# Weights split in 512-column halves, a split-ahead of three products, and a staged, earlier preparation of the token-side sums in a seven-product gate stage

## The chip, the cores and the metric

The kernel runs on one NeuronCore of a Trainium2 chip (eight cores, two dies). The metric is the device time of one execution in microseconds (us). The core's engines run side by side and meet through semaphores: PE (TensorE: matmul, with its weight loads listed apart as PEld), DVE (VectorE), ACT (ScalarE), POOL (GpSimd) and SP (SyncE), which here issues every DMA. Each engine takes its own instructions in the order in which the program issues them.

## The reference

Two layers (DEPTH 2) work on x of 1024 tokens by 1024 channels. Five branches read the same normalised input h; each gives a 1024 x 256 result `yb`; then they are merged:

```python
merged = None
for n, yb in enumerate((y_hg, y_cf, y_sc, y_at, y_mem)):
    term = jax.nn.sigmoid(h @ w_gate[l, n]) * (yb @ w_branch[l, n])
    merged = term if merged is None else merged + term
x = x + rmsnorm(merged @ w_out[l], norm_post[l])
```

`h @ w_gate[l, n]` is a 1024 x 1024 by 1024 x 1024 product for each of five branches and two layers; `h @ w_in[l]` is 1024 x 4352, `yb @ w_branch` 256 x 1024 for each branch. The rest of a layer is a bidirectional linear recurrence (branch 0), a 31-tap depthwise convolution with a layer norm (1), a 3-tap one (2), windowed attention (3) and attention into 256 memory tokens (4). All arrays are float32.

## The kernel before

**Precision.** A float32 product is made of three matmuls in the float32r form. Each operand is split into `hi` (a rounding copy, by ACT) and `lo = x - hi` (a subtraction, by DVE) in `split` (L336); `mm3` adds hi.hi, lo.hi and hi.lo in one PSUM bank. So every weight tile costs one ACT copy and one DVE subtraction before PE can use it, and every 128 x 128 x 512 block of the product costs three matmuls.

**Weights.** `split_w` (L351) makes a `raw` tile (one of four) and issues its load at once; its inner `done` later makes a `hi` and a `lo` tile of 1024 columns (two buffers each) and issues the split. Called with `own`, it takes two long-lived `slot` tiles in their place.

**Items and look-ahead.** `program` (L1459) yields Items, each with a `prep` (issue the loads) and a `body` (issue the matmuls and what reads their result). `drive` (L452) works one item at a time: before an item's body it calls `done` of the next item (the split), then `prep` of the one after that. `plan.wait(need)` holds an item back until a named flag is up.

**The planner.** All five engines are under a manual schedule: the order in which Python issues instructions is the order in which each engine runs them. `Planner` (L117) keeps one clock per engine from rough costs (`Meter`). Work beside the items is a generator handed to `plan.side`: it issues one stage, then yields. After every three matmuls `poll` (L181) issues the next stage of each side whose last stage is finished, by the planner's clocks, at the planner's present PE time. `wait` and `idle` move the planner's PE time on to the next due side; real PE doesn't wait there, only the order of issue is set.

**Buffers.** Long-lived tiles come from 38 `slot`s of 128 x 1024. Short-lived ones of 128 x 512 come from eight `h2` buffers: the terms of the token-side sums, the output copies `pb_out`, the thresholds `th`, and `g_s1`, `g_e`, `g_u` of the gates. A buffer is taken over when every reader of the tile before is done, a DMA included. PSUM has four banks (`mm`) for the items.

**The end of a layer.** After the five branches' own work come, in this order: five pairs of `branch_items` (L1084: 96 matmuls a branch; each 128 x 512 block is copied by ACT to `pb_out` and stored to DRAM as `pb`), mixed with plain gate items (branch 2, and two of branch 0). The last pieces are `cz` (two items of the convolution branch, which need flag `cf`, raised when the convolution's side `conv`, L610, has been issued to its end), one plain gate item `hg_g[1]` (flag `plain`), and the two items of branch 1 (flag `pbs` at their end). Then `strassen_items` (L1209) compute the other 15 gate blocks of 256 columns ("groups"), each as a 2 x 2 block product with seven products in place of eight, in the order P1, P6, P5, P2, P7, P3, P4, each 12 matmuls. The output items (`out_items`, L1371) follow.

**The seven products.** The weight of a group has four blocks a11, a12, a21, a22 in two raw tiles. P1 takes a11, P2 a12, P4 a22; the others take sums: s1 = a21 + a22 for P5, a11' = s1 - a11 for P6, a21' = a11 - a21 for P7, a12' = a12 - a11' for P3. `split_product` (L1227) forms these on DVE in place, when the product is split; products are split into the halves of a shared 1024-column tile pair. On the token side P1, P2 and P3 take blocks of h as they are; P5, P6, P7 and P4 take T1 to T4, sums of blocks of h, made once a layer by the side `gate_forms` (L1162): for i in 0, 1 and k in 0, 1 it rebuilds four blocks (hi + lo), forms four differences and splits them (`put`). The i = 1 half waits for `plain` (slots), its T3 and T4 for `pbs`. P6 of the first group needs flag `forms`, P7 `all_forms`. `after` (L1278) reads each product's bank, applies the gate (tanh) and adds to `mg`; in the last group `halve` (L1267) also makes the split operands of the output product.

Of the kernel before, what the change touches and what calls it, by code (L numbers as in the profile page):

```python
# [12 lines left out]
F32R = mybir.dt.float32r  # L13
# [193 lines left out]
def encoder(ctx: ExitStack, tc: tile.TileContext, a: dict, out: bass.AP):  # L207
# [142 lines left out]

    def split_w(parts, shape, name, own=False):  # L351

        raw = wp.tile(shape, F32, tag="raw", bufs=4, name=f"raw_{name}")
        for dst, src in parts(raw):
            load(out=dst, in_=src)

        def done():
            if own:
                hi, lo = (slot(f"w{v}", F32R).rearrange("p (k c) -> p k c", k=KC) for v in "hl")
            else:  # L360
                hi = wp.tile(shape, F32R, tag="hi", name=f"hi_{name}")
                lo = wp.tile(shape, F32R, tag="lo", name=f"lo_{name}")
            split(hi, lo, raw)
            return hi, lo

        return done

    def cols(l, *starts, own=False):

# [21 lines left out]
    def half_proj(hT, w, s, name):  # L391

        ps = mmt(f"ps_{name}")
        hi, lo = w
        yield from mm3(ps, [(hi[:, k, :], lo[:, k, :], hT[s][0][k // 2][:, k % 2, :], hT[s][1][k // 2][:, k % 2, :])
                            for k in range(KC)])
        return ps

# [132 lines left out]
    def memory_items(l, kv):  # L531

        mT = [None, None]
        plan.side(memory_norm(l, mT))
        src = a["w_mem_kv"][l].rearrange("(k p) c -> p k c", p=P)
        items = []
        for j in range(4):
            def parts(raw, j=j):
                return [(raw, src[:, :, j * P:(j + 1) * P])]

            def prep(j=j, parts=parts):
                return split_w(parts, [P, KC, P], f"mkv{l}{j}")

            def body(w, j=j):
                if j == 0:
                    kv["k"] = slot(f"mK{l}", F32R).rearrange("p (v j m) -> p v j m", v=2, j=2)
                    kv["v"] = small.tile([P, 2, W], F32, tag="mV", bufs=1, name=f"mV{l}")
                ps = mmt(f"ps_mkv{j}")
                yield from mm3(ps[:, :M], [(w[0][:, k, :], w[1][:, k, :], mT[0][k // 4][:, k % 4, :],
                                            mT[1][k // 4][:, k % 4, :]) for k in range(KC)])  # L550
                if j < 2:
                    split(kv["k"][:, 0, j, :], kv["k"][:, 1, j, :], ps[:, :M])
                else:
                    to_tokens(ps[:, :M], kv["v"][:, :, (j - 2) * P:(j - 1) * P])
                yield

            items.append(Item(prep, body, f"mT{l}" if j == 0 else None, f"mkv{l}" if j == 3 else None))
        return items
# [525 lines left out]
    def branch_items(l, n, ys, pbd, need=None, flag=None):  # L1084

        wb = a["w_branch"][l, n].rearrange("(j p) c -> p j c", p=P)
        yT = []
        items = []
        for q in range(2):
            def prep(q=q):  # L1090
                done = split_w(lambda raw: [(raw, wb[:, :, hs(q)])], [P, 2, HALF], f"b{n}{q}")

                def put():
                    if q == 0:
                        plan.wait(need)
                        for j, y in enumerate(ys):
                            yT.append((slot(f"yh{n}{j}", F32R), slot(f"yl{n}{j}", F32R)))
                            split(*yT[j], y)
                    return done()

                return put

            def body(w, q=q):
                for i in range(4):
                    c = slice(i * P, (i + 1) * P)
                    for s in range(2):
                        ps = mmt(f"ps_b{n}")
                        yield from mm3(ps, [(w[0][:, j, c], w[1][:, j, c], yT[j][0][:, hs(s)], yT[j][1][:, hs(s)])
                                            for j in range(2)])
                        pb = h2("pb_out")  # L1110
                        act.copy(out=pb, in_=ps)
                        load(out=pbd[4 * q + i][:, hs(s)], in_=pb)
                        yield

            items.append(Item(prep, body, flag=flag if q else None))
        return items
# [45 lines left out]
    def gate_forms(l, hT, forms):  # L1162
# [17 lines left out]
        for i in range(2):  # L1180
# [2 lines left out]
            dst, late = {}, []  # L1183
            for k in range(2):
                b11, b12, b22, b21 = (h2(f"b{x}") for x in range(4))
                for b, K, s in ((b11, 0, 0), (b12, 0, 1), (b22, 1, 1), (b21, 1, 0)):
                    hi, lo = (hT[s][v][2 * K + i][:, k, :].bitcast(F32) for v in range(2))
                    dve.tensor_tensor(out=b, in0=hi, in1=lo, op=ALU.add)
                dve.tensor_tensor(out=b11, in0=b12, in1=b11, op=ALU.subtract)
                put(dst, 1, k, b11)  # L1190
                dve.tensor_tensor(out=b12, in0=b22, in1=b12, op=ALU.subtract)
                dve.tensor_tensor(out=b22, in0=b22, in1=b11, op=ALU.subtract)
                dve.tensor_tensor(out=b21, in0=b21, in1=b22, op=ALU.subtract)
                put(dst, 2, k, b22)
                yield
                late.append((k, b12, b21))
                if i == 0 or k:
# [3 lines left out]
                    for x, j in ((3, 1), (4, 2)):  # L1201
                        for b in late:
                            put(dst, x, b[0], b[j])
                    late = []
                    yield
        plan.flags.add(f"all_forms{l}")
        yield

    def strassen_items(l, groups, forms, pbd, mg, mgd, mT):  # L1209
# [17 lines left out]
        def split_product(k):  # L1227
            gi, name = k // N, order[k % N]
            r = raws[gi]
            a11, a12, a21, a22 = r[0][:, :4], r[0][:, 4:], r[1][:, :4], r[1][:, 4:]  # L1230
            if name == "P1":
                src = a11
            elif name == "P6":
                s1 = sums[gi] = h2("g_s1").rearrange("p (k c) -> p k c", k=4)
                dve.tensor_tensor(out=s1, in0=a21, in1=a22, op=ALU.add)
                dve.tensor_tensor(out=a21, in0=a11, in1=a21, op=ALU.subtract)
                dve.tensor_tensor(out=a11, in0=s1, in1=a11, op=ALU.subtract)
                src = a11
            elif name == "P5":
                src = sums.pop(gi)  # L1240
            elif name == "P2":
                src = a12
            elif name == "P7":
                src = a21
            elif name == "P3":
                dve.tensor_tensor(out=a12, in0=a12, in1=a11, op=ALU.subtract)
                src = a12
            else:
                src = a22
                raws.pop(gi)  # L1250
            if k % 2 == 0:
                ws["tiles"] = [wp.tile([P, KC, P], F32R, tag=v, name=f"{v}_s{k}") for v in ("hi", "lo")]
            hi, lo = (t[:, 4 * (k % 2):4 * (k % 2) + 4, :] for t in ws["tiles"])
            split(hi, lo, src)
            ws[k] = hi, lo

        def merge(gi, dd, s, th):
            n, g = groups[gi]
# [19 lines left out]
        def after(k):  # L1278
# [40 lines left out]
                flush()  # L1319
                gate(gi, 1, 0, b["E1"])  # L1320
            if gi == len(groups) - 1:
                if name in ("P6", "P5", "P2"):
                    halve(("P6", "P5", "P2").index(name), 0)
                elif name == "P4":
                    flush()
                    halve(3, 0)
# [10 lines left out]
        items = []  # L1337
        for k in range(N * len(groups)):
            def prep(k=k):
                while state["loaded"] < len(groups) and N * state["loaded"] - 5 <= k:  # L1340
                    load_group(state["loaded"])
                    state["loaded"] += 1

                def done():
                    while state["split"] < N * len(groups) and state["split"] <= k + 1:
                        split_product(state["split"])
                        state["split"] += 1

# [22 lines left out]
    def out_items(l, mT, s, x_src, gpost, before, after):  # L1371
# [20 lines left out]
        for cb in range(2):  # L1392
            for q in range(4):
# [3 lines left out]
                def body(w, cb=cb, q=q):  # L1397
# [7 lines left out]
                    for i in range(4):  # L1405
                        if q == 0:
                            pss[i] = mmt("ps_o")
                        if os[i] is None:
# [2 lines left out]
                        ps = pss[i]  # L1411
                        tt = slice(i * P, (i + 1) * P)
                        yield from mm3(ps, [(mT[s][0][q][:, k, tt], mT[s][1][q][:, k, tt],
                                             w[0][:, k, :], w[1][:, k, :]) for k in range(2)],
                                       q == 0, q == 3)
                        if q == 3:
                            junk = h2("osq")
# [10 lines left out]
    with tc.manual_schedule(engines={mybir.EngineType.PE, mybir.EngineType.DVE, mybir.EngineType.Activation,  # L1428
# [30 lines left out]
        def program():  # L1459
# [22 lines left out]
            for l in range(NL):  # L1482
# [8 lines left out]
                else:  # L1491
# [13 lines left out]
                sc_g = [gate_item(l, 2, d, hT, pbd[2], mg[0], mgd[d // 2] if d > 1 else None, True, f"merge{l}")  # L1505
                        for d in range(KC)]
                hg_g = [gate_item(l, 0, d, hT, pbd[0], mg[0], None, False, f"plain{l}" if d else None) for d in range(2)]
                at_b = branch_items(l, 3, y_at, pbd[3], need=f"at{l}")
                mem_b = branch_items(l, 4, y_mem, pbd[4], need=f"mem{l}")
                yield from branch_items(l, 2, y_sc, pbd[2])  # L1510
                yield from sc_g[:1] + branch_items(l, 0, o_hg, pbd[0]) + sc_g[1:3] + at_b + sc_g[3:] + mem_b + hg_g[:1]
                yield from cz + hg_g[1:] + branch_items(l, 1, y_cf, pbd[1], flag=f"pbs{l}")
                groups = [(n, g) for g in range(4) for n in ((3, 4, 1) if g == 0 else (0, 3, 4, 1))]
                forms = {}
                plan.side(gate_forms(l, hT, forms))
                yield from strassen_items(l, groups, forms, pbd, mg, mgd, mT)
                gpost = cache(lambda l=l: row_bcast(a["norm_post"][l], f"gpost{l}"))
                x_src, hT = (x_mid if l else x_in), [None, None]
# [43 lines left out]
```

## Time and profile before

| | us |
|---|---|
| median of 3 runs (2364.68 to 2367.6) | 2365.22 |
| the profiled execution | 2366.64 |
| its span in the trace | 2364.9 |
| mean granted PE clock in the span | 0.989 |
| PE busy (share of the span) | 2276.3 (96%) |
| DVE busy | 1595.1 (67%) |
| ACT busy | 959.8 (41%) |

The span is the time from the first to the last instruction in the trace; 1.7 us of the execution lie outside it. "Busy" is the time in which an engine worked on an instruction; the views behind the page give, for each wait, the instruction that ended it. All kernel code is issued through one helper line (L112), so the views are read by tile name: `ps_b` is the bank of a branch item, `pb_out` its copy, `b` a block of h or a difference of blocks, `T1h`/`T1l` to `T4h`/`T4l` the split sums, `hi_s`/`lo_s` the split weights of a product, `raw_g` a gate weight, `ps_gX`, `ps_gY`, `ps_gZ` the three banks of a group (P1 and P2 in X; P6, P7 and P4 in Y; P5 and P3 in Z).

### The profile page before, as it was taken

The numbers are of one execution on the slowest core, as the hardware profiler recorded it, in microseconds if no ns is written. First come the engines' busy times: TensorE is split into PE (matmuls) and PEld (weight loads), VectorE is DVE, ScalarE is ACT, GpSimd is POOL, SyncE is SP. The second block draws the span as 40 slices with busy tenths as digits, with TensorE's granted clock in tenths as the row PEclk, the third lists the DMA queues.
The fourth block names the chain that finished last, engine by engine and source line by source line (L and its number), as shares of the span: only waits on it lengthen the run. The fifth ranks groups of instructions, "written<-read, shape, count | busy, mean of one in ns | idle before, by whom it ended". The sixth has DMA issues, their size and how long they took to land. (4 is left out here: it accounts for less than half of the span.)

```text
span 2364.9 us, 29886 instructions
## 1 busy us (share of the span) xinstructions
PE 2276.3 (96%) x11560; PEld 1844.3 (78%) x11560; DVE 1595.1 (67%) x2650; ACT 959.8 (41%) x1800; POOL 29.4 (1%) x41
## 2 busy tenths in 40 slices
PE   7999999999998899999999999999999988999998
PEld 6777788888887677777877778888888776777776
DVE  6768645356976777777667685453579667777765
ACT  5333344345344433334442424443543533333342
POOL 1000000000000000000110000000000000000000
PEclk9999999999999899999999999999999999999999
DMA  5210121115542333335430101111245513333334
GB/s 180 86 36 28 40 40 43 45 37 170 177 161 89 135 125 125 107 124 178 160 116 28 36 28 43 28 52 45 76 147 183 192 62 135 125 125 107 103 138 160
DMA packets 248014, 237.31 MB, mean 100 GB/s; under 512 B 29984, under 2 KB 191008, under 8 KB 247872
## 3 DMA queue, kind: packets, MB, share of 16 engines
q1 hardware_dynamic: 247872, 235.40, 30.7%
q8 instruction: 91, 1.49, 0.3%
q14 instruction: 51, 0.42, 0.1%
HBM read 177.69 MB, written 57.67 MB: 100 GB/s over the span
## 5 line engine op out<-in xcount | busy, mean ns | idle before, releaser
L112 DVE TENSOR_TENSOR lo_s<-raw_g,hi_s 128x512 fp32r<-128x512 f32 x180 | 123.9, 688 | 98.0 <-ACT hi_s L112 98.0
L112 DVE SCALAR_TENSOR_TENSOR cf_c<-cf_u,cfw,cf_c 128x1009 f32<-128x1009 f32 (+14 forms) x120 | 153.1, 1276 | 3.2
L112 ACT CAST hi_s<-raw_g 128x512 fp32r<-128x512 f32 x180 | 109.7, 617 | 92.4 <-DVE raw_g L112 88.7
L112 PE MATMUL ps_b<-yh,hi_b 128*128 128x512 f32 x320 | 129.9, 406 | 13.6 <-ACT pb_out L112 13.6
L112 PE MATMUL ps_b<-yh,lo_b 128*128 128x512 f32 x320 | 126.2, 394 | 0.0
L112 PE MATMUL ps_b<-yl,hi_b 128*128 128x512 f32 x320 | 126.2, 394 | 0.0
L112 ACT COPY pb_out<-ps_b 128x512 f32<-128x512 f32 x160 | 91.1, 591 | 68.0 <-PE ps_b L112 49.3
L112 DVE TENSOR_TENSOR lo_in<-raw_in,hi_in 128x1024 fp32r<-128x1024 f32 x60 | 73.3, 1222 | 59.8 <-ACT hi_in L112 54.6
L112 PE MATMUL ps_gX<-h_0h,hi_s 128*128 128x512 f32 x240 | 93.4, 389 | 0.0
L112 PE MATMUL ps_gX<-h_0h,lo_s 128*128 128x512 f32 x240 | 93.4, 389 | 0.0
L112 PE MATMUL ps_gX<-h_0l,hi_s 128*128 128x512 f32 x240 | 93.3, 389 | 0.0
L112 ACT ACTIVATE g_e<-g_e 128x512 f32<-128x512 f32 x60 | 38.0, 634 | 133.0 <-DVE g_e L112 133.0
L112 PEld LDWEIGHTS ps_b<-yh,hi_b 128*128 128x128 f32 x320 | 61.2, 191 | 29.1 <-ACT pb_out L112 15.3
L112 DVE TENSOR_TENSOR lo_wo<-raw_wo,hi_wo 128x1024 fp32r<-128x1024 f32 x32 | 39.0, 1224 | 59.5 <-ACT hi_wo L112 59.5
L112 PEld LDWEIGHTS h_s<-hQQ,hkp 64*128 64x128 f32 x896 | 58.9, 187 | 21.7 <-issue 14.7
L112 DVE COPY_PREDICATED hS<-masks,h_s 128x512 f32<-128x512 uint8 x112 | 75.2, 725 | 0.0
L112 PE MATMUL h_s<-hQQ,hkp 64*128 64x128 f32 x896 | 71.2, 294 | 3.4 <-ACT hkp L112 3.4
L112 ACT CAST hi_in<-raw_in 128x1024 fp32r<-128x1024 f32 x60 | 62.9, 1049 | 27.2 <-issue 26.6
L112 PEld LDWEIGHTS ps_b<-yl,hi_b 128*128 128x128 f32 x320 | 60.9, 190 | 13.2
L112 ACT COPY hkp<-hK 128x512 f32<-128x512 f32 x56 | 37.2, 665 | 83.4 <-DVE hK L112 83.4
L112 PEld LDWEIGHTS ps_b<-yh,lo_b 128*128 128x128 f32 x320 | 61.3, 192 | 11.2
L112 PE MATMUL ps_gY<-T2h,hi_s 128*128 128x512 f32 x120 | 50.8, 423 | 16.5 <-ACT T2h L112 16.5
(557 smaller groups left out, 6531.2 us busy)
## 6 DMA issues: line engine op xcount, KB each, us to landing
raw_g<-in_w_gate_dram SPq DMA_DIRECT2D x80, 512.0 KB, 3.6
pb<-pb_out SPq DMA_DIRECT2D x160, 256.0 KB, 2.3
pb<-pb SPq DMA_DIRECT2D x80, 512.0 KB, 5.0
raw_in<-in_w_in_dram SPq DMA_DIRECT2D x68, 512.0 KB, 3.8
raw_wo<-in_w_out_dram SPq DMA_DIRECT2D x32, 512.0 KB, 4.4
raw_b<-in_w_branch_dram SPq DMA_DIRECT2D x20, 512.0 KB, 5.4
mg<-g_th SPq DMA_DIRECT2D x24, 256.0 KB, 2.1
mg<-mg SPq DMA_DIRECT2D x12, 512.0 KB, 5.5
```

Source lines behind the costliest of these rows:

```text
L112: return f(*args, **kw)
```

## The change

Four things change. (1) `split_w` splits a weight in two halves of 512 columns, each with its own `hi` and `lo` tile (four buffers each), in place of one pass over 1024 columns; it now returns a list of views by k, so that the users index `w[0][k]`. (2) A product of the gate stage has its own pair of 512-column tiles, is split three products ahead (before: two), and a group is loaded one product earlier; the three block sums of a group are formed with P1's split (before: P6's), a12' with P2's (before: P3's). (3) `gate_forms` is handed to the planner before the branch items rather than after them, its stages are cut finer (sums; differences; T1 and T2; T3; T4), and the order of the sums is changed. (4) In the last group `halve` comes one product earlier.

```diff
 def split_w(parts, shape, name, own=False):
...
         def done():
-            if own:
-                hi, lo = (slot(f"w{v}", F32R).rearrange("p (k c) -> p k c", k=KC) for v in "hl")
-            else:
-                hi = wp.tile(shape, F32R, tag="hi", name=f"hi_{name}")
-                lo = wp.tile(shape, F32R, tag="lo", name=f"lo_{name}")
-            split(hi, lo, raw)
-            return hi, lo
+            n, w = shape[1:]
+            flat = raw.rearrange("p k c -> p (k c)")
+            views = [[], []]
+            for s in range(2):
+                if own and s == 0:
+                    halves = [[x[:, hs(s)] for s in range(2)] for x in (slot(f"w{v}", F32R) for v in "hl")]
+                parts = [halves[v][s] if own else split_tile(v) for v in range(2)]
+                split(*parts, flat[:, hs(s)])
+                for v in range(2):
+                    views[v] += [parts[v][:, k * w:(k + 1) * w] for k in range(n // 2)]
+            return views
+
+    def split_tile(v):
+        return wp.tile([P, HALF], F32R, tag=("hi", "lo")[v], bufs=4, name=("hi", "lo")[v])
...
 def gate_forms(l, hT, forms):
...
                 b11, b12, b22, b21 = (h2(f"b{x}") for x in range(4))
-                for b, K, s in ((b11, 0, 0), (b12, 0, 1), (b22, 1, 1), (b21, 1, 0)):
+                for b, K, s in ((b12, 0, 1), (b11, 0, 0), (b22, 1, 1), (b21, 1, 0)):
                     hi, lo = (hT[s][v][2 * K + i][:, k, :].bitcast(F32) for v in range(2))
                     dve.tensor_tensor(out=b, in0=hi, in1=lo, op=ALU.add)
+                yield
                 dve.tensor_tensor(out=b11, in0=b12, in1=b11, op=ALU.subtract)
-                put(dst, 1, k, b11)
                 dve.tensor_tensor(out=b12, in0=b22, in1=b12, op=ALU.subtract)
                 dve.tensor_tensor(out=b22, in0=b22, in1=b11, op=ALU.subtract)
                 dve.tensor_tensor(out=b21, in0=b21, in1=b22, op=ALU.subtract)
+                yield
+                put(dst, 1, k, b11)
                 put(dst, 2, k, b22)
                 yield
                 late.append((k, b12, b21))
...
                     for x, j in ((3, 1), (4, 2)):
                         for b in late:
                             put(dst, x, b[0], b[j])
+                        yield
                     late = []
-                    yield
...
 def split_product(k):
...
+            hi, lo = (split_tile(v).rearrange("p (k c) -> p k c", k=4) for v in range(2))
+            ws[k] = hi, lo
             if name == "P1":
-                src = a11
-            elif name == "P6":
                 s1 = sums[gi] = h2("g_s1").rearrange("p (k c) -> p k c", k=4)
                 dve.tensor_tensor(out=s1, in0=a21, in1=a22, op=ALU.add)
                 dve.tensor_tensor(out=a21, in0=a11, in1=a21, op=ALU.subtract)
+                split(hi, lo, a11)
                 dve.tensor_tensor(out=a11, in0=s1, in1=a11, op=ALU.subtract)
-                src = a11
+            elif name == "P6":
+                split(hi, lo, a11)
...
             elif name == "P2":
-                src = a12
+                split(hi, lo, a12)
+                dve.tensor_tensor(out=a12, in0=a12, in1=a11, op=ALU.subtract)
...
 def after(k):
...
-                if name in ("P6", "P5", "P2"):
-                    halve(("P6", "P5", "P2").index(name), 0)
+                if name in ("P1", "P6", "P5"):
+                    halve(("P1", "P6", "P5").index(name), 0)
...
             def prep(k=k):
-                while state["loaded"] < len(groups) and N * state["loaded"] - 5 <= k:
+                while state["loaded"] < len(groups) and N * state["loaded"] - 6 <= k:
...
-                    while state["split"] < N * len(groups) and state["split"] <= k + 1:
+                    while state["split"] < N * len(groups) and state["split"] <= (k + 2 if k else 1):
...
 def program():
...
+                forms = {}
+                plan.side(gate_forms(l, hT, forms))
                 at_b = branch_items(l, 3, y_at, pbd[3], need=f"at{l}")
...
                 yield from cz + hg_g[1:] + branch_items(l, 1, y_cf, pbd[1], flag=f"pbs{l}")
                 groups = [(n, g) for g in range(4) for n in ((3, 4, 1) if g == 0 else (0, 3, 4, 1))]
-                forms = {}
-                plan.side(gate_forms(l, hT, forms))
```

More of the change, by code (lines that the diff above doesn't have):

```diff
@@ L394, in half_proj @@
         hi, lo = w
-        yield from mm3(ps, [(hi[:, k, :], lo[:, k, :], hT[s][0][k // 2][:, k % 2, :], hT[s][1][k // 2][:, k % 2, :])
+        yield from mm3(ps, [(hi[k], lo[k], hT[s][0][k // 2][:, k % 2, :], hT[s][1][k // 2][:, k % 2, :])
                             for k in range(KC)])
@@ L548, in body @@
                 ps = mmt(f"ps_mkv{j}")
-                yield from mm3(ps[:, :M], [(w[0][:, k, :], w[1][:, k, :], mT[0][k // 4][:, k % 4, :],
+                yield from mm3(ps[:, :M], [(w[0][k], w[1][k], mT[0][k // 4][:, k % 4, :],
                                             mT[1][k // 4][:, k % 4, :]) for k in range(KC)])
@@ L1107, in body @@
                         ps = mmt(f"ps_b{n}")
-                        yield from mm3(ps, [(w[0][:, j, c], w[1][:, j, c], yT[j][0][:, hs(s)], yT[j][1][:, hs(s)])
+                        yield from mm3(ps, [(w[0][j][:, c], w[1][j][:, c], yT[j][0][:, hs(s)], yT[j][1][:, hs(s)])
                                             for j in range(2)])
@@ L1236, in split_product @@
                 dve.tensor_tensor(out=a21, in0=a11, in1=a21, op=ALU.subtract)
+                split(hi, lo, a11)
                 dve.tensor_tensor(out=a11, in0=s1, in1=a11, op=ALU.subtract)
-                src = a11
+            elif name == "P6":
+                split(hi, lo, a11)
             elif name == "P5":
-                src = sums.pop(gi)
+                split(hi, lo, sums.pop(gi))
             elif name == "P2":
-                src = a12
+                split(hi, lo, a12)
+                dve.tensor_tensor(out=a12, in0=a12, in1=a11, op=ALU.subtract)
             elif name == "P7":
-                src = a21
+                split(hi, lo, a21)
             elif name == "P3":
-                dve.tensor_tensor(out=a12, in0=a12, in1=a11, op=ALU.subtract)
-                src = a12
-            else:
[L1249 to L1255, printed above, removed]
+                split(hi, lo, a12)
+            else:
+                split(hi, lo, raws.pop(gi)[1][:, 4:])
         def merge(gi, dd, s, th):
@@ L1413, in body @@
                         yield from mm3(ps, [(mT[s][0][q][:, k, tt], mT[s][1][q][:, k, tt],
-                                             w[0][:, k, :], w[1][:, k, :]) for k in range(2)],
+                                             w[0][k], w[1][k]) for k in range(2)],
                                        q == 0, q == 3)
```

## The prediction, made before the changed kernel had run

> **What bounds the kernel now.** I read the page first, then PE's waits, then the busy times in stretches cut at PE's own stages, and last the chain and the timelines inside the stretches that lose time.
>
> ```profile
> PE 2276.3 (96%) x11560; PEld 1844.3 (78%) x11560; DVE 1595.1 (67%) x2650; ACT 959.8 (41%) x1800; POOL 29.4 (1%) x41
> ```
>
> PE is the bound, so only PE's gaps can be won. Its waits (total us, times, longest):
>
> ```profile
> PE ps_gY L112 <- ACT T2h L112: 16.5, 2, 8.3
> PE ps_b L112 <- ACT pb_out L112: 13.6, 4, 4.7
> ...
> PE ps_gY L112 <- DVE lo_s L112: 6.3, 28, 0.2
> ...
> PE ps_o L112 <- ACT hi_wo L112: 4.3, 4, 1.2
> ```
>
> The largest two, the most frequent one and the one at the output items all lie where the change works: in the gates, their approach and their exit. Next the stretches (elapsed; PE, PEld, DVE, ACT, POOL busy; granted clock): cz and one plain gate item, branch 1, P1 and P6 of the first group, the rest of it, 60 us of steady groups.
>
> ```profile
> 723.50:756.20 32.70, 32.70 (x146) 27.04 (x146) 21.15 (x25) 11.84 (x15) 0.00 (x0) 1.00 0.11 33
> 756.20:787.30 31.10, 24.29 (x97) 19.33 (x96) 23.93 (x37) 14.35 (x26) 0.00 (x0) 0.89 0.31 117
> 787.30:802.00 14.70, 6.44 (x26) 4.89 (x26) 12.08 (x20) 6.49 (x13) 0.00 (x0) 0.75 0.57 182
> 802.00:821.70 19.70, 19.48 (x79) 15.43 (x78) 13.80 (x22) 6.21 (x12) 0.00 (x0) 0.92 0.33 107
> 900.00:960.00 60.00, 59.31 (x256) 47.61 (x256) 46.97 (x74) 22.62 (x40) 0.00 (x0) 1.00 0.36 123
> ```
>
> The chain through a steady group gives PE's unit and the stall:
>
> ```profile
> 2007.70 2.79 PE ps_gY L112 x11
> 2010.49 2.72 PE ps_gZ L112 x12
> ...
> 2027.52 2.83 PE ps_gY L112 x11
> ...
> 2245.48 2.81 PE ps_gY L112 x11
> ```
>
> A product takes 2.72 us, a matmul 0.227. Twelve groups take 2245.48 - 2007.70 = 237.8, or 19.81 each; seven products are 19.04. So 0.77 per group is lost, at P6: from P7's end (2010.49 + 3 x 2.72 = 2018.7) to P6's start (2027.5) the DVE queue runs the additions of `after`, three block sums and at last P6's lo_s, 8.8 us, and PE has only P3, P4 and P1 (8.16) to cover it. Branch 1 needs 96 x 0.227 = 21.8 and takes 31.1; P1 and P6 need 5.4 and take 14.7; the rest of the group loses (1 - 0.92) x 19.7 = 1.6 to the clock. Together 20 us: the **approach**; both layers have it, as the two waits for T2h show.
>
> **The change part by part.**
>
> *Split-ahead and sums at P1.* P6's split is now issued three products before its use and holds no sums. P1's split holds them, also three products ahead: 8.16 us for three sums and a split, with less queued ahead. DVE's total per group is unchanged, 46.97 x 19.81/60 = 15.5 us by the last stretch, of 19.04 in a shorter group, so no new bound. A split's ACT copy now waits for the product four back, which has just ended when `after` has run, so nothing more is queued behind it than before. The raw load is one product earlier on SP; it waits only for buffers that P4's earlier split frees sooner. Gain 14 x 0.75 x 2 layers = **-21**. Bounds: nothing (the queue stays late) to -22.
>
> *Halves of 512.*
>
> ```profile
> L112 DVE TENSOR_TENSOR lo_s<-raw_g,hi_s 128x512 fp32r<-128x512 f32 x180 | 123.9, 688 | 98.0 <-ACT hi_s L112 98.0
> ...
> L112 ACT CAST hi_s<-raw_g 128x512 fp32r<-128x512 f32 x180 | 109.7, 617 | 92.4 <-DVE raw_g L112 88.7
> ...
> L112 DVE TENSOR_TENSOR lo_in<-raw_in,hi_in 128x1024 fp32r<-128x1024 f32 x60 | 73.3, 1222 | 59.8 <-ACT hi_in L112 54.6
> ```
>
> Per weight DVE pays 2 x 0.688 - 1.222 = 0.15 more and ACT 2 x 0.617 - 1.04 = 0.19 (1.04: hi_wo below). A layer splits 74 weights (34 w_in, 4 memory, 10 branch, 10 gate, 16 output); for 148 that is 22 and 28 us of engine time. Items of 48 matmuls (10.9 us) hide it. Without that cover it would cost 22; a first half ready 0.5 earlier could also win a microsecond. The nearest row without cover is the convolution's tail, a serial DVE chain before cz: I take **+2**.
>
> [...]
>
> *Exit to the output items.*
>
> ```profile
> 2262.24 1.04 ACT hi_wo L112
> 2263.30 1.23 DVE lo_wo L112
> ...
> 2271.18 1.23 DVE lo_wo L112
> 2272.45 81.72 PE ps_o L112 x352
> ```
>
> The last group's P6 starts at 2245.48, so P4 ends at 2245.48 + 2.81 + 5 x 2.72 = 2261.9; PE waits for hi_wo to 2263.3, lo_wo to 2264.5, and the second weight (2272.45 against 2264.5 + 23 x 0.227 = 2269.7): 1.4 + 1.2 + 2.7. Halves bring the first hi 0.4 and the first lo 1.0 sooner, and halve() off DVE's last 10 us brings U2's add sooner by about a microsecond. The first two waits nearly go; the third stays, since the chain E1, merges, halve, lo_wo is the same. **-3 per layer, -6.** Bounds 0 to -10.
>
> *Forms as staged side work.* This decides the size. Today the four blocks of forms (call them F1 to F4) start inside branch 1. ACT's in-order queue sits behind T1h and T2h (13.6 of PE's wait), then P6 waits for F4's T2h (16.5).
>
> ```profile
> 735.22 0.69 DVE L112 SCALAR_TENSOR_TENSOR cf_c<-cf_t,cf_c 128x512 f32<-128x512 f32 x1
> ...
> 759.56 0.69 DVE L112 TENSOR_TENSOR b<-h_0h,h_0l 128x512 f32<-128x512 f32 x1
> 760.16 1.28 DVE L112 TENSOR_TENSOR b<-h_1h,h_1l 128x512 f32<-128x512 f32 x2
> ...
> 763.94 2.14 DVE L112 TENSOR_TENSOR b<-b,b 128x512 f32<-128x512 f32 x3
> ```
>
> ```profile
> 799.87 0.62 ACT L112 CAST T2h<-b 128x512 fp32r<-128x512 f32 x1 [2.09 <-DVE b L112]
> ```
>
> In the new order they start when flag cf rises, which is the end of the tail on DVE (735.9), while PE began cz at 723.5: PE is 12 us ahead of the planner there. DVE's queue from then to F4's T2l: per block four sums at 0.61 (759.56 to 760.16), four differences 0.61 + 2.14, T1l and T2l 1.2, so 6.4; four blocks 25.6; T3, T4 of F1 and F2 2.4; cz's eight updates 5.3; lo_g, yl and two lo_b 6.2; four updates of the plain item 2.7; four splits and four sums 5.2. Sum 47.4: 783.3. P6's last quarter is due at 756.2 + 21.8 + 2.7 + 2.0 = 782.7. On DVE alone the wait would be gone.
>
> Two things speak against it. First, lo_g now stands behind F1 (7.6 with its T3 and T4), two updates (2.7) and F2's sums (2.4): its first half is ready at 749.2, where PE, done with cz's 96 matmuls, wants it at 745.5: 3.7 lost, and a half-rate stretch perhaps (1.7, about the 1.6 seen above). Second, the **eight h2 buffers**. Working through the planner's costs by hand for the order only, F4's sums are issued between the ninth and the tenth pb_out of branch 1. From there F3's two late terms, F4's four and g_s1 (held until P5's split, after branch 1) make seven. One buffer is left for pb_out 10 to 16, and each must wait for the store of the one before:
>
> ```profile
> L112 ACT COPY pb_out<-ps_b x16: 578/589/621, 765.9 to 791.3; 128x512 f32<-128x512 f32 x16
> ...
> DMA to landing us min/median/max: 2.0/2.2/4.5
> ```
>
> (pb_out in this stretch: least, median and longest.) That ACT has to wait for such a store is a row of the view of all pb_out, four times:
>
> ```profile
>   DMA pb<-pb_out: 3.1, 4
> ```
>
> A turn is 0.59 + 2.0 + 0.06 = 2.65 us; PE makes a block in 1.36. pb_out 9 stands behind P6's hi_s, which waits for the block sums: the part of the sum above that stands ahead of it is 38.5 (774.4), and some 3 us of waits for ACT come on top: 777.5, an estimate. Seven turns later it is 796.0; then hi_s of P5 and P2, T1h and T2h at 0.62 each: 798.5, and T2l a little before 800. Today T2h is done at 800.5 (799.87 + 0.62). The stall changes its name (ps_b, then ps_g, on pb_out and its DMA), and little is won: **-1 per layer, -2**, bounds -13.5 (no buffer wait) to +12 (turns at the 4.5 us landing).
>
> The sum: -21 + 2 - 6 - 2 = -27 us. The profiled execution (2366.6) would become 2339.6; it lies 1.4 above the median 2365.2, so the median becomes **2338**.
>
> **The rivals.**
>
> *A. The approach empties.* If F4's sums come after most pb_outs, or buffers turn faster, only 6.5 of the 20 us per layer stay (3.7 + 1.7 + about 1 of ACT order). For it: DVE's sum fits. Against: the count of seven. A further -25: 2313.
>
> *B. Slower.* The same buffer wait, with slow stores: the next group's two raw loads (128 x 1024 float32, 512 KB each) are now issued before branch 1's last eight stores. The row's longest landing is 4.5, so a turn would be 5.15: seven turns cost 7 x 2.5 = 17.5 more per layer than forecast, 2373. It decides at turns of 4.6 us, where the 27 are gone. Against: the median landing is 2.2.
>
> *C. Not what it says.* P6's wait stays, because DVE, in order, is still late with its split, whatever was issued ahead: -21 falls away, 2359. For: DVE's chain was 8.8 us long. Against: 3.5 us of slack in each group.
>
> [...]
>
> **How the numbers follow.** Forecast 0.58, A 0.25, C 0.09, B 0.08. About 0.2% (4.7 us) is what a measurement of this kernel can tell from no change: below 2360.5 lie the forecast, A and two thirds of C, 0.88; within it 0.05; above, most of B, 0.07. The range runs from A's lower side, 2310 (A's price is uncertain by some 6 us), to C's 2361; B and a part of A stay out, under 0.17. The forecast's own range is 2327 to 2347.
>
> **What would show it.** Steady groups of 19.04 us and no row "ps_gY <- DVE lo_s" confirm the first part; 19.8 is C. In the approach, F4's T2h at its old distance behind cz and pb_out spaced at 2.6 us or more confirm the buffer wait; T2h 10 us earlier is A. A wait at ps_g for lo_g near cz's end shows the late plain gate. ps_o's first two waits should go and the third stay. The forecast is wrong above all if F4's sums are issued later than I read the order, or if the halves disturb the recurrence's stages, where DVE and PE take turns.

## The result and the profile after

The changed kernel takes 2349.05 us (median of 4 runs, 2344.22 to 2350.51) beside 2366.41 for the kernel before on the same chip: a ratio of 0.9922, 95% interval 0.9905 to 0.994. It is 17.4 us faster where 27 were forecast. The profiled execution is the slowest of the four, 2350.51 with a span of 2348.7. First the page's row of busy times, then PE's waits (us in total, times, longest) in the changed kernel:

```profile
PE 2265.9 (96%) x11560; PEld 1848.2 (79%) x11560; DVE 1603.2 (68%) x2798; ACT 973.4 (41%) x1948; POOL 26.8 (1%) x41
```

```profile
PE ps_gY L112 <- ACT T2h L112: 10.1, 2, 5.1
...
PE ps_g L112 <- DVE lo L112: 7.2, 2, 3.6
PE ps_b L112 <- ACT pb_out L112: 7.0, 6, 1.7
...
PE ps_o L112 <- ACT hi L112: 1.9, 2, 1.0
...
PE ps_o L112 <- DVE lo L112: 1.6, 2, 0.8
```

The 148 more instructions on DVE and on ACT are the second halves of 74 weights in each of two layers. The row ps_gY <- DVE lo_s (28 times) is gone, the two waits at the output items have halved, T2h's is smaller, and a wait of the plain gate item for its lo is new.

The chain of waits of the changed kernel through the last layer's groups and its exit (start, us, what; every product is a row of 2.72):

```profile
2100.40 2.72 PE ps_gY L112 x12
...
2233.68 2.72 PE ps_gY L112 x12
...
2241.84 2.73 PE ps_gY L112 x12
2248.58 0.61 ACT hi L112
2249.26 1.29 DVE lo L112 x2
2257.21 0.69 DVE lo L112
2257.95 78.72 PE ps_o L112 x346
```

From P6 at 2100.40 to P6 at 2233.68 lie seven groups: 133.28 / 7 = 19.04 each, against 19.81 before. Over 28 groups that is 0.75 x 28 = 21 us. At the exit P7 starts at 2241.84, so P4 ends at 2241.84 + 2.73 + 2 x 2.72 = 2250.0, and PE goes on without a stop from the second output weight on, at 2257.95: 7.95 later. Before, the same stretch took 2272.45 - 2261.9 = 10.55.

Now the stretches of the approach (elapsed; PE, PEld, DVE, ACT, POOL busy; granted clock): cz, the plain gate item, branch 1, P1 and P6, the rest of the first group; at last 60 us of steady groups.

```profile
735.80:757.58 21.78, 21.78 (x97) 18.02 (x96) 19.03 (x27) 10.13 (x15) 0.00 (x0) 1.00 0.08 24
757.58:773.97 16.39, 12.80 (x49) 10.08 (x48) 16.15 (x25) 6.40 (x10) 0.00 (x0) 0.90 0.12 33
773.97:801.30 27.33, 22.83 (x97) 17.60 (x95) 18.11 (x29) 11.12 (x20) 0.00 (x0) 1.00 0.44 154
801.30:813.74 12.44, 6.90 (x24) 4.84 (x25) 3.83 (x7) 5.87 (x11) 0.00 (x0) 0.87 0.44 155
813.74:829.04 15.30, 15.30 (x62) 12.47 (x60) 12.08 (x20) 6.15 (x11) 0.00 (x0) 0.88 0.44 148
900.00:960.00 60.00, 60.00 (x266) 49.73 (x265) 49.12 (x77) 23.25 (x41) 0.00 (x0) 1.00 0.39 136
```

PE's first matmul of cz and of the second group's P1 in the timelines, before (first fence) and after (second):

```profile
723.54 0.40 PE L112 MATMUL ps_cz<-h_0h,hi_in 128*128 128x512 f32 x1
...
817.00 0.39 PE L112 MATMUL ps_gX<-h_0h,hi_s 128*128 128x512 f32 x1
```

```profile
735.80 0.40 PE L112 MATMUL ps_cz<-h_0h,hi 128*128 128x512 f32 x1
...
829.04 0.39 PE L112 MATMUL ps_gX<-h_0h,hi 128*128 128x512 f32 x1
```

Two things are to be seen. The approach takes 93.24 us where it took 93.46 (93.27 and 93.58 in layer 1): its loss has moved, and almost none of it has gone. At 0.227 a matmul the plain gate item loses 16.39 - 48 x 0.227 = 5.5, branch 1 27.33 - 96 x 0.227 = 5.5, P1 and P6 12.44 - 24 x 0.227 = 7.0 and the rest 15.30 - 60 x 0.227 = 1.7, together 19.7. And cz starts **12.3 us later** than before. The groups, the exits and the approach are close to the forecast; what the forecast lacks is this delay, some 600 us ahead of the place where the gain is made. The windows between 60 and 100 us show where it arises, before (first) and after (second):

```profile
60.00:80.00 20.00, 18.91 (x115) 13.74 (x112) 15.48 (x28) 6.36 (x14) 0.00 (x0) 0.91 0.14 46
80.00:100.00 20.00, 20.00 (x155) 17.30 (x156) 14.99 (x25) 7.05 (x12) 0.00 (x0) 1.00 0.55 152
```

```profile
60.00:80.00 20.00, 14.66 (x86) 10.55 (x86) 16.21 (x29) 5.96 (x14) 0.00 (x0) 0.74 0.20 66
80.00:100.00 20.00, 17.96 (x135) 14.74 (x134) 12.82 (x24) 5.55 (x11) 0.00 (x0) 1.00 0.42 119
```

Taken as one window, these 40 us hold 219 matmuls and transposes in place of 268, and the clock falls to 0.74 in the first half of it. This is the opening of layer 0, where the recurrence, the position bias and the memory's norm run as sides beside the first items.

### The profile page after: what moved, and what is told of

Its sections match the earlier page's. It is cut to its first block, busy times and chain, and to the rows that moved or that the text cites. A ratio compares the mean times of both kernels' runs of the same rounds, so it can differ in the third digit from the quotient of the medians.

```text
span 2348.7 us, 30484 instructions
## 1 busy us (share of the span) xinstructions
PE 2265.9 (96%) x11560; PEld 1848.2 (79%) x11560; DVE 1603.2 (68%) x2798; ACT 973.4 (41%) x1948; POOL 26.8 (1%) x41
## 4 chain that ended last, share of the span: by engine, by line
PE 86%; DVE 7%; ACT 3%; issue 2%; DMA 2%; SPq 0%; POOL 0%; DVEq 0%; ACTq 0%; POOLq 0%
PE ps_gY L112 10%; PE ps_g L112 9%; PE ps_b L112 8%; PE ps_o L112 7%; PE ps_gZ L112 7%; PE ps_gX L112 7%; PE ps_hf L112 4%; PE h_s L112 3%; PE ps_hi L112 2%; PE ps_cb L112 2%; PE ps_hq L112 2%; PE ps_ca L112 2%; PE ps_at_z L112 2%; PE ps_sz L112 2%; PE ps_hz L112 2%; PE ps_sc L112 2%
## 5 line engine op out<-in xcount | busy, mean ns | idle before, releaser
L112 DVE TENSOR_TENSOR lo<-raw_g,hi 128x512 fp32r<-128x512 f32 x220 | 149.5, 687 | 95.7 <-ACT hi L112 95.5
L112 ACT CAST hi<-raw_g 128x512 fp32r<-128x512 f32 x220 | 133.5, 616 | 49.2 <-PE ps_gY L112 44.2
L112 PE MATMUL ps_b<-yh,hi 128*128 128x512 f32 x320 | 127.8, 399 | 7.0 <-ACT pb_out L112 7.0
L112 PE MATMUL ps_b<-yl,hi 128*128 128x512 f32 x320 | 124.8, 390 | 0.0
L112 PE MATMUL ps_b<-yh,lo 128*128 128x512 f32 x320 | 124.8, 390 | 0.0
L112 DVE TENSOR_TENSOR lo<-raw_in,hi 128x512 fp32r<-128x512 f32 x120 | 77.3, 686 | 48.6 <-ACT hi L112 48.4
L112 PE MATMUL ps_gX<-h_0h,hi 128*128 128x512 f32 x240 | 93.6, 390 | 2.5 <-ACT pb_out L112 2.5
L112 PE MATMUL ps_gX<-h_0l,hi 128*128 128x512 f32 x240 | 93.4, 389 | 0.0
L112 PE MATMUL ps_gX<-h_0h,lo 128*128 128x512 f32 x240 | 93.4, 389 | 0.0
L112 ACT CAST hi<-raw_in 128x512 fp32r<-128x512 f32 x120 | 69.0, 620 | 26.4 <-PE ps_ca L112 13.1
L112 PEld LDWEIGHTS ps_b<-yh,lo 128*128 128x128 f32 x320 | 60.2, 188 | 11.1
```

The costliest lines, as they stand in the source:

```text
L112: return f(*args, **kw)
```

## The experiments

**Why is the opening late?** Two theories. **T**: the halves' added engine time (by the forecast 0.15 us on DVE and 0.19 on ACT for each weight) falls where nothing covers it. **O**: the order. `Meter` charges two passes of 512 columns more than one of 1024, and a matmul waits, in the planner's books, only for its half; so the planner's clocks move and it deals out the side stages of the opening in another order. Four kernels separate the engine work from the order. The kernel before ran again beside each set of runs and took 2366.4 to 2367.9 us, so a difference between kernels of two sets carries some 1.5 us of error beside the spread of their own runs.

*e1*: the kernel before with `split_w` of the changed kernel and a pair of 512-column tiles for each product; nothing else.

> The kernel before with the first part of the change alone (weights split in halves of 512 columns; a product of the gate stage has its own pair of 512-column tiles). In the trace of the changed kernel, layer 0's cz starts 12.3 us later than before (735.8 against 723.5) and layer 1 loses 1.7 more, and both theories put this on the halves: 2366.4 + 14 - 3 (the first waits at the output items get shorter, as they did) = about 2377, cz of layer 0 near 735. If cz of layer 0 starts near 723.5, the loss comes from another part of the change, and both theories fall.

*e2*: the same instructions, charged as one pass:

```diff
...
-                split(*parts, flat[:, hs(s)])
+                nc.scalar.copy(out=parts[0], in_=flat[:, hs(s)])
+                nc.vector.tensor_tensor(out=parts[1], in0=flat[:, hs(s)], in1=parts[0].bitcast(F32), op=ALU.subtract)
+                names += [x.tensor.name for x in parts]
+                if s == 1:
+                    plan.add("ACT", 0.055 + T * 0.00087, names[::2], [raw.tensor.name])
+                    plan.add("DVE", 0.065 + T * 0.00107, names[1::2], [raw.tensor.name] + names[::2])
```

> As e1, but the planner is charged for a weight's split as for one pass over 1024 columns, so that PE's matmuls stand in the order of the kernel before; the instructions are those of e1. Theory O (the loss is the order: the halves' costs made the planner issue the opening of layer 0 in another order): cz of layer 0 within 3 us of 723.5 and a time of 2363 to 2367. Theory T (the loss is the added engine time, 0.15 us on DVE and 0.19 us on ACT for each weight, in a stretch without cover): as e1, about 2377, cz near 735.

*e3*: the reverse, the kernel before with one pass per weight, charged as two:

```diff
-            split(hi, lo, raw)
+            nc.scalar.copy(out=hi, in_=raw)
+            nc.vector.tensor_tensor(out=lo, in0=raw, in1=hi.bitcast(F32), op=ALU.subtract)
...
+            for s in range(2):
+                h, o = (x if own else f"{x}/{s}" for x in (hi_, lo_))
+                plan.add("ACT", 0.055 + HALF * 0.00087, [h], [raw_])
+                plan.add("DVE", 0.065 + HALF * 0.00107, [o], [raw_, h])
...
```

The rest of this edit lets a matmul wait, in the planner's books, only for the half that it reads.

> The kernel before, each weight split in one pass as there, but the planner charged as for two halves, so that PE's matmuls stand in the order of e1. Theory O: cz of layer 0 some 12 us late, about 2366.4 + 14 = 2380. Theory T: no more engine time, so 2366 and cz near 723.5.

*e4*: e2's edit on the changed kernel.

> The changed kernel with the planner charged for a weight's split as for one pass, so that PE's matmuls stand in the order of the kernel before. Theory O: the 12 to 14 us come back: 2349 - 13 = about 2336, near the 2338 that was predicted. Theory T: 2349, as the changed kernel.

| | PE's order of before | PE's new order |
|---|---|---|
| one pass per weight | 2367.89 (before) | 2384.83 (e3), ratio 1.0072 (1.0059 to 1.0086) |
| halves | 2363.16 (e2), ratio 0.9976 (0.9968 to 0.9985) | 2377.11 (e1), ratio 1.0039 (1.0027 to 1.0052) |
| halves and the other parts | 2337.94 (e4), ratio 0.9873 (0.9859 to 0.9886) | 2349.05 (the changed kernel) |

PE's records show that e2 and e4 have the order of the kernel before, and e1 and e3 that of the changed kernel. O holds in each row and T in none: the order alone costs 16.9, 14.0 and 11.1 us. The halves themselves win 4.7 (e2) or 7.7 (e1 against e3), where T had them cost time. The engine time that T rests on was priced too high as well: from before to e2 DVE's busy time grows by 9.0 us (1595.1 to 1604.1) and ACT's by 14.2 (959.8 to 974.0), not by 22 and 28. Two halves issued back to back overlap: they take 1.27 or 1.29 us on DVE (the rows lo<-raw_mkv below), where one pass took 1.22. cz of layer 0 starts at 723.04 in e2 and 723.96 in e4, at 735.95 in e1 and 735.26 in e3. The DVE timelines of e1 (first) and e2 (second) show one place of the new order:

```profile
53.31 1.29 DVE L112 TENSOR_TENSOR lo<-raw_mkv,hi 128x512 fp32r<-128x512 f32 x2 [3.68 <-ACT hi L112]
54.52 0.62 DVE L112 CAST masks<-masks_f 128x896 uint8<-128x896 f32 x1
...
55.39 0.68 DVE L112 TENSOR_SCALAR hK<-hF 128x1024 f32<-128x1024 f32 x1
```

```profile
51.93 0.62 DVE L112 CAST masks<-masks_f 128x896 uint8<-128x896 f32 x1
52.46 0.69 DVE L112 TENSOR_SCALAR hK<-hF 128x1024 f32<-128x1024 f32 x1
...
56.52 1.27 DVE L366 TENSOR_TENSOR lo<-raw_mkv,hi 128x512 fp32r<-128x512 f32 x2
```

In e1 the memory's first weight is split ahead of the recurrence's masks and hK. DVE stands 3.68 us behind ACT's hi, and the recurrence starts 2.9 us later (hK 55.39 against 52.46), though PE is 2.4 ahead of e2 up to there (ps_hi at 46.53 and 48.90). Then the item's matmuls are used up while the sides still need DVE. The windows of e1 and e2 show it:

```profile
60.00:80.00 20.00, 15.74 (x69) 10.91 (x68) 14.79 (x27) 6.05 (x14) 0.00 (x0) 0.58 0.20 66
```

```profile
60.00:80.00 20.00, 19.22 (x127) 14.18 (x128) 15.85 (x31) 6.45 (x15) 0.00 (x0) 1.00 0.11 41
```

PE and DVE take turns, PE does half as many instructions, and at a clock of 0.58. That the one pair of rows above is the whole cause was not tried. Where the time goes can be counted, since e1 and e2 issue the same 11560 instructions on PE. The 240th starts 1.1 us earlier in e1 than in e2 (62.5 and 63.6 us), the 540th 10.8 later (116.1 and 105.3), the 1500th 9.9 later (259 us in e2), the 2890th, just ahead of the branch items, 12.4 later, and the last 13.8 later.

*e11* asks whether the loss lies in the opening: e4's charge for the first twelve weights only (`whole = plan.splits <= 12`).

> As e4, but only the first twelve weights (layer 0's first eight and the four of the memory) are charged as one pass; from there on the planner is charged for halves as in the changed kernel. PE's order is that of the kernel before in the first 840 instructions and another one behind them. If the loss sits in the opening, it is e4's time, 2338, at most 2340. If the later places of the order count as much, it lies halfway or nearer to the changed kernel, 2343 to 2349.

2342.23 us (2338.29 to 2344.99, ratio 0.99, 0.9883 to 0.9916). In the profiled execution, the fastest, cz of layer 0 is back at 723.18 and the time is 2338.29, e4's. By the median 6.8 of the 11.1 are back; so by both the opening holds most of the loss. The runs spread over 6.7 us, too far to tell the rest by their times. The same count in the traces shows it: between PE's 1500th and 2890th instruction (259 to 514 us) e1 loses 2.5 us more to e2, and the changed kernel and e11 2.4 each to e4. So the later order costs a part too; e11's profiled execution hides it, because it is 3.7 us ahead of e4 by the 300th instruction.

**What holds the approach?** The ACT timeline of the changed kernel, from P6's hi on:

```profile
788.86 0.62 ACT L112 CAST hi<-raw_g 128x512 fp32r<-128x512 f32 x1 [2.49 <-DVE raw_g L112]
789.38 0.58 ACT L112 COPY pb_out<-ps_b 128x512 f32<-128x512 f32 x1
792.40 0.58 ACT L112 COPY pb_out<-ps_b 128x512 f32<-128x512 f32 x1 [2.44 <-DMA pb<-pb_out]
795.10 0.58 ACT L112 COPY pb_out<-ps_b 128x512 f32<-128x512 f32 x1 [2.11 <-DMA pb<-pb_out]
...
808.74 0.58 ACT L112 COPY pb_out<-ps_b 128x512 f32<-128x512 f32 x1 [2.08 <-DMA pb<-pb_out]
...
810.77 0.62 ACT L112 CAST T2h<-b 128x512 fp32r<-128x512 f32 x1
```

One copy every 2.7 us, each behind the store of the one before: the single buffer of the forecast, and T2h 2 us behind the last. The new wait of the plain gate item, in DVE's timeline:

```profile
758.41 0.68 DVE L112 TENSOR_TENSOR b<-h_1h,h_1l 128x512 f32<-128x512 f32 x1
...
760.22 0.68 DVE L112 TENSOR_TENSOR b<-h_0h,h_0l 128x512 f32<-128x512 f32 x1
760.82 1.28 DVE L112 TENSOR_TENSOR lo<-raw_g,hi 128x512 fp32r<-128x512 f32 x2
```

PE has wanted that lo since 757.6; F2's four sums stand ahead of it. The next four kernels change the buffers and this order, alone and together.

*e5*: `bufs=9` for h2 (the counts of the tiny tiles of `sml` go from 16 to 14, 8 and 4 to make room).

> The changed kernel with nine h2 buffers instead of eight (the room comes from the buffer counts of tiles of up to 32 bytes); no instruction is added or moved. Buffer theory: seven are held from F4's sums on, so two are left for pb_out 10 to 16, a turn of 2.65 us then covers two blocks (1.33 each, PE makes one in 1.36), the row ps_b <- pb_out of branch 1 and P6's wait for T2h go: 2 x (5.5 + 6.8 + 1) = 27 less, 2349 - 27 = about 2322. Rival: T2h is late because DVE's own queue is, as ahead of the change; the wait moves from ps_b to P6 and the time stays at 2349. In between: branch 1's part goes and P6's stays (or grows), about 2338.

*e6*: F2 waits for a flag that the plain item's split raises:

```diff
             def done():
                 pb = slot("pb")
                 load(out=pb, in_=pbd[d])
-                return gate(), pb
+                w = gate()
+                if flag:
+                    plan.flags.add(f"go_{flag}")
+                return w, pb
...
             for k in range(2):
+                if k and not i:
+                    yield f"go_plain{l}"
```

> The changed kernel with F2 (the second block of the token-side sums) held back until the split of the plain gate item's weight has been issued: on DVE its two lo_g stand ahead of F2's four sums and nothing else moves. The wait of ps_g for lo (3.6 a layer) falls by four sums of 0.61, to 1.2, and with it perhaps the half-rate stretch (5.4 in all lost there). If P6's T2h hangs on the turns of pb_out, what PE gains there it loses again at ps_b or ps_gY: 2349, no less than 2346. If T2h moves with PE, 2349 - 2 x 4 = 2341.

*e7*: both. *e8*: both, and e4's charge.

> Both edits, nine h2 buffers and lo_g ahead of F2's sums, on the changed kernel. Buffer theory: with the turns gone nothing takes the gain back, so the two add up: 2322 - 2 x 4 = 2314. Rival (DVE's queue sets T2h): P6 waits the longer, as in e5, 2349 to 2338.

> As e7, with the planner charged for a weight's split as for one pass (e4), so that the opening keeps the order of the kernel before. The opening and the approach lie 600 us apart, so the gains add up: 2337.9 - 27 - 8 = about 2303 by the buffer theory; 2338 to 2327 by its rival.

| | median us (runs) | ratio to before, 95% |
|---|---|---|
| changed kernel | 2349.05 (2344.22 to 2350.51) | 0.9922 (0.9905 to 0.994) |
| e5 nine h2 | 2334.97 (2329.81 to 2338.35) | 0.9863 (0.9848 to 0.9877) |
| e6 lo first | 2348.79 (2346.09 to 2350.58) | 0.9922 (0.9908 to 0.9935) |
| e7 nine, lo first | 2328.88 (2326.33 to 2331.65) | 0.9839 (0.9825 to 0.9852) |
| e8 and the old order | 2316.17 (2311.73 to 2317.75) | 0.9782 (0.9769 to 0.9795) |

A ninth buffer, with no instruction added or moved, wins 14.1 us, so the rival, under which the time stays, is out. By its time alone e5 lies nearer to the case in between (2338) than to the buffer theory (2322); its waits, below, decide for the buffers. By the medians e6 alone wins nothing (0.3) and 6.1 once the ninth buffer is there, though the intervals of e5 and e7 still touch. e6's profiled execution shows a small gain: the two approaches take 91.24 and 90.11 us, 2.0 and 3.2 less than in the changed kernel, so a few us may hide in the spread of its four runs. In e6's waits the plain item's went from 7.2 to 2.3, and branch 1, reached earlier, waits longer (6.5 + 2.6 for 7.0); T2h's wait stays as it was:

```profile
PE ps_gY L112 <- ACT T2h L112: 10.1, 2, 5.1
...
PE ps_b L112 <- ACT pb_out L112: 6.5, 6, 1.4
...
PE ps_b L112 <- DVE lo L112: 2.6, 2, 1.3
...
PE ps_g L112 <- DVE lo L112: 2.3, 2, 1.2
```

By the medians e5 fell short of the 27 by half. Its waits (there is no row ps_b <- pb_out any more) and its ACT timeline say why:

```profile
PE ps_g L112 <- DVE lo L112: 9.8, 2, 4.9
...
PE ps_gY L112 <- ACT T2h L112: 2.5, 2, 2.1
...
PE ps_gY L112 <- DVE T2l L112: 1.9, 2, 1.0
```

```profile
787.88 0.62 ACT L112 CAST hi<-raw_g 128x512 fp32r<-128x512 f32 x1 [2.49 <-DVE raw_g L112]
788.41 1.06 ACT L112 COPY pb_out<-ps_b 128x512 f32<-128x512 f32 x2
791.54 1.19 ACT L112 COPY pb_out<-ps_b 128x512 f32<-128x512 f32 x2 [2.07 <-DMA pb<-pb_out]
794.26 0.59 ACT L112 COPY pb_out<-ps_b 128x512 f32<-128x512 f32 x1 [1.53 <-DMA pb<-pb_out]
796.71 1.07 ACT L112 COPY pb_out<-ps_b 128x512 f32<-128x512 f32 x2 [1.86 <-DMA pb<-pb_out]
799.40 0.59 ACT L112 COPY pb_out<-ps_b 128x512 f32<-128x512 f32 x1 [1.62 <-DMA pb<-pb_out]
...
801.45 0.62 ACT L112 CAST T2h<-b 128x512 fp32r<-128x512 f32 x1
```

The copies still start late, behind P6's hi, and the eight from 788.41 to 799.40 start 1.57 us apart, where 1.33 were expected of two buffers and PE makes a block in 1.36. PE no longer waits at ps_b, presumably because its banks cover the lag, but T2h stays 2 us behind the last copy. And in layer 0 PE comes 2.3 us earlier to the plain item, whose lo lets it go on only 1.0 earlier: 9.8 in place of 7.2. Nor did I expect how far the four runs lie apart. The profiled one, 2329.81, is the fastest of them, so its span is 20.7 below that of the changed kernel, while the medians give 14.1. Of the 20.7 the two approaches hold 19.1 (84.26 and 83.17 us in place of 93.24 and 93.27). Another 2.3 lie far ahead of them: in the first 40 us the clock is 1.00 here and 0.91 in the changed kernel's profiled execution.

e8 beats both kernels: 50.5 us below the kernel before, 2.9 times the gain of the change. e7 and e8 miss the 2314 and 2303 expected by 15 and 13 us, as e5 misses its 2322 by 13, so the same shortfall runs through the three.

**What are the other parts worth?** *e9* puts the split of a product back to two ahead, the sums to P6 and P3, the load to its old place. *e10* hands `gate_forms` over behind the branch items again:

```diff
-                forms = {}
-                plan.side(gate_forms(l, hT, forms))
                 at_b = branch_items(l, 3, y_at, pbd[3], need=f"at{l}")
...
                 groups = [(n, g) for g in range(4) for n in ((3, 4, 1) if g == 0 else (0, 3, 4, 1))]
+                forms = {}
+                plan.side(gate_forms(l, hT, forms))
```

> The changed kernel with its second part undone: a product is split two products ahead, the three block sums stand with P6's split and a12' with P3's, and a group is loaded as late as before. If the 0.75 us of a group come from P6's late split alone, the row ps_gY <- DVE lo_s (here lo) is back 28 times and the time is 2349 + 28 x 0.72 = about 2369. If the steady groups gain from something else (the halves' own tiles, the finer stages), they stay at 19.04 and the time at 2349.

> The changed kernel with the token-side sums handed to the planner behind the branch items, as before (their finer stages stay). The prediction priced the earlier hand-over at 1 us a layer, the traces of before and after show 0.4: 2350 to 2351, the loss of the approach back in two waits, ps_b on pb_out and ps_gY on T2h, and none at ps_g for lo. If the hand-over carries more than the two approaches' sums show, 2355 or more; if it cost time (the late lo_g, the turns of pb_out), 2345 or less.

e9 takes 2370.72 us (ratio to before 1.0014, 1.0005 to 1.0023), 21.7 above the changed kernel, and the wait for lo is back; e10 takes 2350.75 (0.9934, 0.9922 to 0.9947), 1.7 above it, as expected, but too little to tell from no change: the intervals overlap. The row that answers, in PE's waits of e9 (first; the weight's low part is named lo here) and of e10 (second):

```profile
PE ps_gY L112 <- DVE lo L112: 6.4, 28, 0.2
```

```profile
PE ps_gY L112 <- ACT T2h L112: 26.0, 6, 5.5
```

In e10 there is no wait for lo at ps_g and, against what I expected, none at ps_b: the whole loss of the approach stands in one place, T2h. Its approach takes 93.68 us in layer 0, beside 93.46 before and 93.24 in the changed kernel. Three arrangements of the same side work lose the same 20 us a layer in different places.

## Why the prediction was right, and where it was wrong

**Split-ahead, -21: right, in cause and size.** The groups take 19.04, and undoing this part alone costs 21.7 (e9). Rival C is out.

**Exit, -6: right in cause, a little short in size.** PE goes on behind P4 without a wait in both layers, so the first two waits are gone; the third, for the second weight's hi and lo (0.96 and 0.81 us in each layer), stays. Counted from the start of P4's last matmul to the end of that wait, the stretch falls from 10.7 to 8.3 us in both layers: 2.4 each where 3 were forecast. Behind it PE ran at half rate for 3.4 us in both layers before (matmuls 0.43 us apart; a clock of 0.51 from 2272.86 to 2276.20), and does so in layer 0 alone now, which adds a gain that was not forecast. Over both layers ps_o's waits for hi and lo fall from 7.2 to 3.5; with the halves alone (e2) they are 5.2. The earlier `halve` was not run by itself.

**Approach, -2: right that little is won, and why.** The traces give 0.2 in layer 0 and 0.3 in layer 1; undoing the move costs 1.7, which is not clear of the noise, so the size is not shown. The late lo_g cost 3.6 (forecast 3.7) and a half-rate stretch, by the loss of the plain gate item 5.5 - 3.6 = 1.9 in layer 0 (1.7 in the forecast); the turns are 2.7 (2.65), and it is the last seven pb_out that take them, as counted. The upper bound of this step is a slip: at the 4.5 us landing rival B's own price, 17.5, would make it +16.5, not +12. Nothing rests on it, since the turns stayed at 2.7. The rival that the approach empties (A) names the same buffers as its condition, and e5 shows them to be the condition, though one more buffer gave half of A's price.

**Halves of 512, +2: wrong, and with it the sum.** That step costed the halves by engine time, looked for the place where it would be uncovered, and named the convolution's tail. Run alone they cost 9.2 (e1): 4.7 gained by themselves and 14.0 lost by the order, some 10 of it in the first 260 us. The price by engine time was too high in itself: mean durations of 0.69 and 1.22 give 0.15 a weight on DVE, but the 60 weights of lo_in take 73.3 us whole and 77.3 halved in the changed kernel (x120, a mean of 0.686), 0.07 each. The working for the approach used the planner's costs "for the order only"; the same was needed at each of the 74 weights of a layer, because a change in what the planner is charged moves work that the diff doesn't touch. The warning at the end named the right place, the recurrence's stages, where DVE and PE take turns, but gave it no price and no mechanism; the turns are there, and what brings them on is the order of issue.

Three of the four parts, as run, come to +9.2 - 21.7 - 1.7 = -14.2 of the measured -17.4; the 3.2 between hold the earlier `halve` and the errors of three differences of a few us each. With the old order restored (e4) the changed kernel takes 2337.94, where the forecast of 2338 had assumed that order without saying so. That the two agree to a tenth is luck: e4 is 30 below its own kernel before for 27 forecast, and in it the halves win 4.7 where the sum has them cost 2. Of the halves' own 4.7, 2.0 are the shorter waits at the output items; where the rest comes from is not shown (e2's profiled execution is the slowest of its eleven).

## What to carry to other kernels

Where a planner issues the work, its cost table is a part of the program: when an instruction is cut in two, compare the order of issue before and after through the whole kernel, and price that apart from the instructions (here +14 against -5). When a wait hangs on a ring of buffers, count what is held while the transient tiles turn; one buffer of 256 KB won as much as the order lost, and moving work ahead of that wait won nothing by the medians until the ring was wider. Undo each part of a change alone: here -22, -2 and +9 hid behind a single -17.

## What the runs showed of the hardware

PE ran at half rate behind a wait of 2.5 us. In e7 (PE timeline) the matmuls that follow it take 0.43 us from start to start for 3.4 us, in place of 0.23:

```profile
761.59 0.50 PE L112 MATMUL ps_g<-h_0h,lo 128*128 128x512 f32 x1 [2.51 <-DVE lo L112]
...
762.45 0.63 PE L112 MATMUL ps_g<-h_0h,lo 128*128 128x512 f32 x1
762.88 0.63 PE L112 MATMUL ps_g<-h_0l,hi 128*128 128x512 f32 x1
```

The changed kernel shows the same in both layers, behind waits of 3.59 and 3.57 us for the same lo: 0.43 from start to start, and a granted clock of 0.52 from 762.94 to 766.24 us in layer 0. In e6, where F2's sums no longer stand ahead of lo, the wait is 1.2 us, and the clock stays at 1.00 through the item. But the length of a wait doesn't decide alone. In e7 P6 of the first group waits 2.4 us for T2h in layer 0, and the clock stays at 1.00 behind it. At the exit of the changed kernel PE waits 0.96 us for the second output weight's hi and 0.81 for its lo, in both layers; in the 3.4 us behind them the clock is 0.50 in layer 0 (1104.05 to 1107.45) and 1.00 in layer 1 (2258.28 to 2261.69). What decides is not shown. The runs of e5 differ in the clock as they do in time: 2329.81 us at a mean granted clock of 0.993, and 2332.91 to 2338.35 at 0.989 to 0.990.
